# A latent attention block whose softmax reciprocals go through DRAM, with its closing steps tied to places in the engines' queues

## The chip, the cores and the metric

The kernel runs on one core of a Trainium2 chip. The metric is the device time of one execution in microseconds (us). The kernel before takes 1403.3 us, the median of three runs from 1401.08 to 1404.21. The core's engines are named as the profile names them: PE (TensorE, matrix products; PEld is its weight load), DVE (VectorE), ACT (ScalarE), POOL (GpSimd) and SP (SyncE, which here only issues DMAs). Each engine takes its instructions in the order of its own queue; semaphores make it wait for the others.

## What is computed

One layer of a bidirectional encoder over S = 2048 tokens of width 1024. One input projection feeds two groups of mixers: gated linear attention in chunks, forward and backward, and latent attention with a low-rank key and value and a rotary part. Their outputs, side by side, go through one output projection; a scaled residual and a layer norm follow. The part that the change touches is the second:

```python
def mla_branch(c_q, c_kv, k_rope, gate, positions, q_norm_g, w_uq, kv_norm_g, w_ukv):
    ...
    kv = (rms_norm(c_kv, kv_norm_g) @ w_ukv).reshape(B, S, MLA_HEADS, MLA_D_NOPE + MLA_DV)
    ...
    q_rope = apply_rope(q[..., MLA_D_NOPE:], positions) * scale
    k_nope, v = kv[..., :MLA_D_NOPE], kv[..., MLA_D_NOPE:]
    ...
        s = (jnp.einsum('bqhd,bkhd->bhqk', qn, k_nope, preferred_element_type=jnp.float32)
             + jnp.einsum('bqhr,bkr->bhqk', qr, k_r, preferred_element_type=jnp.float32))
        p = jax.nn.softmax(s, axis=-1)
        return jnp.einsum('bhqk,bkhv->bqhv', p.astype(v.dtype), v)
    ...
    return o * jax.nn.silu(gate)
```

There are 4 heads, 2048 queries and 2048 keys; a key has 128 numbers without position and 64 rotary ones, a value 128.

## The kernel before, in words

Most products are split to keep close to float32 at the speed of fp32r: a matrix A is a high part in float32r (A rounded by a copy on ACT, `hi`) and a low part (A minus its high part, on DVE or POOL, `lo`), and `mm3` makes three fp32r matmuls of them, high by high, high by low and low by high (L82 to L84). A plain float32 matmul is one call and appears as two rows.

The span has four stages. Up to about 385 us, `sweep_a` projects the 16 chunks of 128 tokens for the linear attention and runs its backward scan. On the way it makes the cos and sin tables of the rotary part (`rope_tables`), which lie in a pool that lives as long as the kernel. From about 385 to 400, `late_gates` loads the weights of the next projection (`wzr`, eight DMAs) and builds the remaining gates. From about 395 to 676, `sweep_c` makes the latents, the queries, the gates and the forward scan in eight steps of two chunks; its first matmuls of the scan (Ob, L792) follow on the first projections (ipm). It leaves queries in DRAM (`qh_s`, `ql_s`, `rh_s`, `rl_s`), gates in `gm_s`, the other group's outputs in `oa_s`. From about 676, `attention` (L894) runs 16 blocks: for each of 4 groups of 512 queries, each of 4 heads. The output projection of 16 chunks (`OutProj`, L1085) overlaps the last blocks and then runs alone to the end.

A block handles 512 queries of one head against all keys, in 8 pairs of key tiles (2 x 128 keys, against 512 columns of queries).

- `s_pair` (L929): ten fp32r matmuls make the scores of a pair in PSUM (L937 to L941; two buffers of two banks). ACT copies them to SBUF (L943), DVE keeps a running maximum over the pairs (L948).
- `maxima` (L951): DVE folds the two halves, PE transposes four times (mx, L958), DVE takes the maximum over the partitions (L960), and PE transposes it back, spread over all partitions (mb, L963), into a bank of the pool pM.
- `pv_pair` (L967): DVE subtracts mb (L970), ACT takes the exponential (L971). ACT and DVE or POOL split it into ph and pl (L65, L71), PE multiplies by the latent values into the bank o (L82 to L84; in mode "n" with one plain float32 matmul, L988). POOL adds the exponentials up in acc (L984). PV_MODE "dpdpndpd" says who makes pl for each of the 8 pairs: DVE (d), POOL (p), or nobody (n).
- `finish` (L1000): ACT copies o to osb (L1004), POOL folds acc (L1006). PE transposes the fold (sx, L1010), DVE sums it over the partitions and takes reciprocals (L1012, L1013), PE transposes those back, spread (r, L1017), DVE multiplies osb by r (L1018). PE multiplies by the head's value matrix wv (y, L1021), DVE multiplies by the gate (gma, L1023, loaded by L926 a block ahead), and the product is stored to `ob_s` (L1024).

Three pairs after the scores of a block have ended (LEAD = 3), its `pv_pair` steps begin, beside the scores of the next block. `finish` is a generator of four pieces; `todo` and FIN = (0, 2, 4) say after which later `pv_pair` each piece is emitted.

The order in each engine's queue isn't that of the program: the framework orders the instructions of each engine by a list schedule over their dependencies and buffers. `after` (L72 and on) pins the instructions made in it behind a given one. In `pv_pair` such a pin puts a pair's acc behind pl on POOL in block 0 alone (L983). The pools of PSUM hold two banks for mb (pM), one for o (pO), one for mx, sx, r and y (pX) and four for the scores (pS). `OutProj` takes its banks from pS and from pM (L1050, L1135). SP issues the loads of q (`fetch`, L911), of gma (`start`, L923) and of wo (L1038) in its queue's order.

The matrix wv is loaded and scaled in `setup_q` (L244), before the attention.

Of the kernel before, what the change touches and what calls it, by code (L numbers as in the profile page):

```python
# [9 lines left out]
F32 = mybir.dt.float32  # L10
F32R = mybir.dt.float32r
# [45 lines left out]
class K:  # L57
# [22 lines left out]
    def mm3(self, out, ah, al, bh, bl, start=True, stop=True):  # L80
        mm = self.nc.tensor.matmul
        mm(out, ah, bh, start=start, stop=False)  # L82
        mm(out, ah, bl, start=False, stop=False)  # L83
        mm(out, al, bh, start=False, stop=stop)  # L84
# [66 lines left out]
    def run(self):  # L151
        tc, nc, ins = self.tc, self.nc, self.ins
        with ExitStack() as top:
# [10 lines left out]
            self.oa_s = [dp.tile([P, H, P], F32, name=f"oa_s{c}") for c in range(NCH)]  # L164
            self.ob_s = [dp.tile([P, H, QB], F32, name=f"ob_s{b}") for b in range(NQB)]
# [5 lines left out]
            self.wv = cp.tile([P, H * P], F32, name="wv")  # L171
            self.cos = cp.tile([P, NCH, 32], F32, name="cosT")
            self.sin = cp.tile([P, NCH, 2, 32], F32, name="sinT")
# [35 lines left out]
    def setup_q(self, w1, ps):  # L209
# [15 lines left out]
        nc.sync.dma_start(self.wv, ins["wv"])  # L225
# [18 lines left out]
        nc.scalar.activation(self.wv, self.wv, AF.Copy, scale=self.gkv_c[:, 0:1])  # L244
# [48 lines left out]

    def rope_tables(self, hpi):
# [6 lines left out]
        V.tensor_scalar(self.sin[:, :, 0, :], self.sin[:, :, 1, :], -1.0, None, ALU.mult)  # L301


    def sweep_a(self):
        tc, nc, ins, cp = self.tc, self.nc, self.ins, self.cp
        with ExitStack() as ctx:
# [16 lines left out]
            hpi = wp.tile([P, 1], F32, name="hpi")  # L323
            nc.scalar.preload_act_table_set(EXP_LN)
# [260 lines left out]
    def late_gates(self):  # L585

        tc, nc, ins, bc = self.tc, self.nc, self.ins, self.bc
        self.xch = bc.tile([P, NK, 2, P], F32R, name="xch")
# [305 lines left out]
    def attention(self):  # L894
# [5 lines left out]
        with ExitStack() as ctx:  # L900
# [3 lines left out]
            pM = ctx.enter_context(tc.tile_pool(name="pM", bufs=2, space=PSUM, reuse_waits="tile"))  # L904
            pO = ctx.enter_context(tc.tile_pool(name="pO", bufs=1, space=PSUM, reuse_waits="tile"))
# [17 lines left out]
            def start(i):  # L923
                h, b = blocks[i]
                gm = bp.tile([P, QB], F32, tag="gm", name=f"gma{i}")
                nc.sync.dma_start(gm, self.gm_s[b][:, h])  # L926
                stt[i].update(gm=gm)

            def s_pair(i, j):  # L929
# [13 lines left out]
                d["copy"] = Ac.activation(s, ps, AF.Copy).ins  # L943
                src = s if i == 0 else ps
                if j > 0:
                    if j == 1:
                        d["rm"] = self.xfp.tile([P, 2, QB], F32, tag="xf", name=f"rm{i}")
                    V.tensor_tensor(d["rm"], src, d["s"][0] if j == 1 else d["rm"], ALU.max)  # L948
# [18 lines left out]
            def pv_pair(i, j):  # L967
# [10 lines left out]
                if j == 0:  # L978
                    d["acc"] = acc = bp.tile([P, 2, QB], F32, tag="acc", name=f"acc{i}")
# [257 lines left out]
```

## Time and profile before

| | us |
|---|---|
| median of 3 runs | 1403.3 |
| lowest and highest | 1401.08, 1404.21 |
| the profiled execution's own time | 1405.04 |
| its span in the trace | 1403.2 |
| PE busy | 1336.0 |
| DVE, ACT, POOL busy | 1021.5, 792.1, 693.1 |
| mean granted TensorE clock of the core | 0.983 |

The span runs from the first to the last instruction in the trace; the execution's own time holds some 2 us more. The prediction shows lines of several views. A row of a timeline has the start and the length of an instruction, its engine, line and operation, what it writes and reads, and in brackets how long its engine had been idle, with what ended that time. Matmuls overlap, and their lengths are modelled, so the distance between two starts says more than the length. A row of the waits has the engine and line that waited, what it waited for, the total, the number and the longest. The chain of waits follows the work back from its end, at each step to what released it. Line numbers are those of the kernel before; a number such as L71 can be that of a helper that many steps call.

### The profile page before, as it was taken

The numbers are of one execution on the slowest core, as the hardware profiler recorded it, in microseconds if no ns is written. First come the engines' busy times: TensorE is split into PE (matmuls) and PEld (weight loads), VectorE is DVE, ScalarE is ACT, GpSimd is POOL, SyncE is SP. The second block draws the span as 40 slices with busy tenths as digits, with TensorE's granted clock in tenths as the row PEclk, the third lists the DMA queues.
The fourth block names the chain that finished last, engine by engine and source line by source line (L and its number), as shares of the span: only waits on it lengthen the run. The fifth ranks groups of instructions, "written<-read, shape, count | busy, mean of one in ns | idle before, by whom it ended". The sixth has DMA issues, their size and how long they took to land.

```text
span 1403.2 us, 19420 instructions
## 1 busy us (share of the span) xinstructions
PE 1336.0 (95%) x7072; PEld 1139.4 (81%) x7072; DVE 1021.5 (73%) x1655; ACT 792.1 (56%) x1302; POOL 693.1 (49%) x353
## 2 busy tenths in 40 slices
PE   6899999999989999899999999999999999899997
PEld 6799999999888888888877777777777777678886
DVE  7747764545598777777588888888887789967665
ACT  6555556555565555655566777767666668521100
POOL 2432424232342222231088888888888888662210
PEclk9899999999999999999999999999999999999999
DMA  7222222222565555553821111111111002064432
GB/s 246 87 67 70 66 70 66 71 69 68 178 219 166 173 173 158 173 165 108 270 95 46 46 46 45 45 46 45 45 46 41 20 23 61 16 207 168 143 117 72
DMA packets 85297, 141.56 MB, mean 101 GB/s; under 512 B 9070, under 2 KB 38126, under 8 KB 85200
## 3 DMA queue, kind: packets, MB, share of 16 engines
q1 hardware_dynamic: 84528, 138.21, 31.7%
q0 software_dynamic: 672, 2.10, 0.4%
q8 instruction: 56, 0.92, 0.3%
q14 instruction: 41, 0.34, 0.1%
HBM read 89.95 MB, written 50.33 MB: 100 GB/s over the span
## 4 chain that ended last, share of the span: by engine, by line
PE 38%; DVE 11%; POOL 10%; issue 6%; ACT 5%; DMA 2%; SPq 0%; DVEq 0%; POOLq 0%; ACTq 0%
POOL acc L984 7%; POOL pl L71 3%; DVE MMb L71 2%; PE pS L940 2%; PE pS L941 2%; PE pS L937 2%; PE pS L939 2%; PE pS L938 2%; PE o L83 2%; PE o L84 2%; PE po L82 2%; PE po L84 2%; PE po L83 2%; PE pn L82 2%; PE pn L84 2%
## 5 line engine op out<-in xcount | busy, mean ns | idle before, releaser
L984 POOL TENSOR_TENSOR acc<-acc,s 128x1024 f32<-128x1024 f32 x96 | 269.8, 2811 | 13.4 <-ACT s L971 9.5
L943 ACT ACTIVATE s<-pS 128x1024 f32<-128x1024 f32 x128 | 131.2, 1025 | 108.8 <-PE pS L941 107.3
L970 DVE TENSOR_TENSOR s<-s,mb 128x1024 f32<-128x1024 f32 x128 | 152.9, 1206 | 12.3 <-PE mb L963 12.3
L65 ACT ACTIVATE ph<-s 128x1024 fp32r<-128x1024 f32 x112 | 118.2, 1055 | 44.8 <-PE o L84 44.5
L71 POOL TENSOR_TENSOR pl<-s,ph 128x1024 fp32r<-128x1024 f32 x43 | 109.4, 2544 | 68.4 <-ACT ph L65 68.4
L948 DVE TENSOR_TENSOR rm<-pS,rm 128x1024 f32<-128x1024 f32 x90 | 109.3, 1215 | 40.3 <-ACT s L943 40.3
L82 PE MATMUL ipa<-wah,xah 128*128 128x384 f32 (+1 forms) x384 | 130.8, 341 | 7.0 <-ACT wah L65 7.0
L971 ACT ACTIVATE s<-s 128x1024 f32<-128x1024 f32 x128 | 132.9, 1049 | 5.0 <-DVE s L970 5.0
L71 DVE TENSOR_TENSOR pl<-s,ph 128x1024 fp32r<-128x1024 f32 x69 | 116.3, 1685 | 16.3 <-ACT ph L65 16.1
L84 PE MATMUL ipa<-wah,xal 128*128 128x384 f32 (+1 forms) x384 | 125.9, 328 | 0.0
L83 PE MATMUL ipa<-wal,xah 128*128 128x384 f32 (+1 forms) x384 | 125.5, 327 | 0.2 <-DVE wal L71 0.2
L575 POOL TENSOR_TENSOR Us<-Us,cw 128x512 f32<-128x512 f32 x16 | 18.2, 1138 | 202.0 <-DVE Us L572 172.6
L937 PE MATMUL pS<-qh,ckvT_h 128*128 128x512 f32 x256 | 115.0, 449 | 0.0
L940 PE MATMUL pS<-rh,krs 128*128 128x512 f32 x256 | 101.4, 396 | 0.0
L939 PE MATMUL pS<-qh,ckvT_l 128*128 128x512 f32 x256 | 101.2, 395 | 0.0
L938 PE MATMUL pS<-ql,ckvT_h 128*128 128x512 f32 x256 | 101.0, 395 | 0.0
L941 PE MATMUL pS<-rl,krs 128*128 128x512 f32 x256 | 101.0, 395 | 0.0
L83 PE MATMUL o<-pl,vh 128*128 128x512 f32 x224 | 92.0, 411 | 7.0 <-DVE pl L71 4.0
L82 PE MATMUL o<-ph,vh 128*128 128x512 f32 x224 | 90.3, 403 | 0.8 <-ACT ph L65 0.8
L84 PE MATMUL o<-ph,vl 128*128 128x512 f32 x224 | 89.9, 401 | 0.0
L71 POOL TENSOR_TENSOR ol<-of,oh 128x512 fp32r<-128x512 f32 x32 | 44.5, 1403 | 81.0 <-PE po L84 63.0
L82 PEld LDWEIGHTS ipa<-wah,xah 128*128 128x128 f32 x384 | 73.5, 191 | 7.9 <-ACT wah L65 7.2
(311 smaller groups left out, 3900.4 us busy)
## 6 DMA issues: line engine op xcount, KB each, us to landing
xcf<-xT_dram SPq DMA_DIRECT2D x16, 512.0 KB, 4.0
xr<-x_dram SPq DMA_DIRECT2D x16, 512.0 KB, 3.8
out_dram<-rr SPq DMA_DIRECT2D x32, 256.0 KB, 2.1
xaf<-xT_dram SPq DMA_DIRECT2D x14, 512.0 KB, 4.2
SU<-su_s SPq DMA_DIRECT2D x16, 256.0 KB, 4.1
qdb<-qd_s SPq DMA_DIRECT2D x16, 256.0 KB, 4.5
oib<-oi_s SPq DMA_DIRECT2D x16, 256.0 KB, 2.6
ub<-u_s SPq DMA_DIRECT2D x16, 256.0 KB, 3.0
```

The costliest lines, as they stand in the source:

```text
L71: return e.tensor_tensor(dst, src, hi.bitcast(F32), ALU.subtract).ins
L82: mm(out, ah, bh, start=start, stop=False)
L83: mm(out, ah, bl, start=False, stop=False)
L84: mm(out, al, bh, start=False, stop=stop)
L937: mm(ps[:, e], kh, qh, start=True, stop=False)
L938: mm(ps[:, e], kh, ql, start=False, stop=False)
L939: mm(ps[:, e], kl, qh, start=False, stop=False)
L940: mm(ps[:, e], kr, rh, start=False, stop=False)
L943: d["copy"] = Ac.activation(s, ps, AF.Copy).ins
L970: V.tensor_tensor(s, s, d["mb"][:, None, :].to_broadcast([P, 2, QB]), ALU.subtract)
L971: Ac.activation(s, s, AF.Exp)
L984: d["pool"] = G.tensor_tensor(d["acc"], d["s0"] if j == 1 else d["acc"], s, ALU.add).ins
```

## The change

- **The close of a block.** The transposes r are gone. The reciprocals (rc, 128 x 4) are stored to DRAM (`r_s`, 512 numbers in a row) and loaded again, spread over all partitions (rb). o is split into a high part (ACT) and a low part (DVE), y is an `mm3` of three fp32r matmuls with a split wv, and the reciprocals are multiplied into the gate (gm*rb) in place of osb.
- **Ties.** `mm3` returns its last matmul. The last score copy on ACT (`cpi`), the last running maximum on DVE (`mxi`) and the last value matmul on PE (`pvi`) are kept, and the pieces of `finish` are pinned behind them: the high part of o behind cpi, sx behind pvi, y and gm*rb behind pvi and mxi. The fold is emitted ahead of the last pair's matmuls; the other pieces come 1 and 7 pairs later. A pair's acc is pinned behind pl for every "p" pair of all blocks.
- **Banks.** pM has one bank, pO two; `OutProj` takes its bank from pO.
- **Tables and weights.** cos and sin are made in a pool of `sweep_a`, stored to DRAM (`rope_s`, 768 KB) and loaded again in `late_gates`. wv is loaded, scaled and split at the start of the attention. gm is loaded in `finish`, in one buffer.

```diff
@@ -81,7 +81,7 @@
         mm(out, ah, bl, start=False, stop=False)
-        mm(out, al, bh, start=False, stop=stop)
+        return mm(out, al, bh, start=False, stop=stop).ins
 
@@ -162,15 +162,14 @@
             self.oa_s = [dp.tile([P, H, P], F32, name=f"oa_s{c}") for c in range(NCH)]
+            self.rope_s = [dp.tile([P, NCH, n, 32], F32, name=f"rope_s{n}") for n in (1, 2)]
+            self.r_s = [dp.tile([1, QB], F32, name=f"r_s{i}") for i in range(NQB * H)]
             self.ob_s = [dp.tile([P, H, QB], F32, name=f"ob_s{b}") for b in range(NQB)]
...
             self.gn_c = cp.tile([P, 1], F32, name="gn_c")
-            self.wv = cp.tile([P, H * P], F32, name="wv")
-            self.cos = cp.tile([P, NCH, 32], F32, name="cosT")
-            self.sin = cp.tile([P, NCH, 2, 32], F32, name="sinT")
             self.cw = cp.tile([P, NCH, 3, H], F32, name="cw")
@@ -222,7 +221,6 @@
         nc.sync.dma_start(wqT, ins["wqT"])
-        nc.sync.dma_start(self.wv, ins["wv"])
         nc.vector.tensor_scalar(gq, gq, QK_SCALE, None, ALU.mult)
@@ -241,7 +239,6 @@
             self.lo(self.wabs_l[:, ct], wa, self.wabs_h[:, ct], "pool")
-        nc.scalar.activation(self.wv, self.wv, AF.Copy, scale=self.gkv_c[:, 0:1])
         yield
@@ -291,6 +288,10 @@
 
+    def rope_tiles(self, pool, name):
+        self.cos = pool.tile([P, NCH, 32], F32, name=f"cos{name}")
+        self.sin = pool.tile([P, NCH, 2, 32], F32, name=f"sin{name}")
+
     def rope_tables(self, hpi):
@@ -299,6 +300,8 @@
         V.tensor_scalar(self.sin[:, :, 0, :], self.sin[:, :, 1, :], -1.0, None, ALU.mult)
+        nc.sync.dma_start(self.rope_s[0][:, :, 0], self.cos)
+        nc.sync.dma_start(self.rope_s[1], self.sin)
 
@@ -321,6 +324,7 @@
             hpi = wp.tile([P, 1], F32, name="hpi")
+            self.rope_tiles(wp, "T")
             nc.scalar.preload_act_table_set(EXP_LN)
@@ -585,6 +589,9 @@
         tc, nc, ins, bc = self.tc, self.nc, self.ins, self.bc
+        self.rope_tiles(bc, "C")
+        nc.sync.dma_start(self.cos, self.rope_s[0][:, :, 0])
+        nc.sync.dma_start(self.sin, self.rope_s[1])
         self.xch = bc.tile([P, NK, 2, P], F32R, name="xch")
@@ -901,8 +908,8 @@
             bp = ctx.enter_context(tc.tile_pool(name="bp", bufs=2, reuse_waits="tile"))
-            pM = ctx.enter_context(tc.tile_pool(name="pM", bufs=2, space=PSUM, reuse_waits="tile"))
-            pO = ctx.enter_context(tc.tile_pool(name="pO", bufs=1, space=PSUM, reuse_waits="tile"))
+            pM = ctx.enter_context(tc.tile_pool(name="pM", bufs=1, space=PSUM, reuse_waits="tile"))
+            pO = ctx.enter_context(tc.tile_pool(name="pO", bufs=2, space=PSUM, reuse_waits="tile"))
             pX = ctx.enter_context(tc.tile_pool(name="pX", bufs=1, space=PSUM, reuse_waits="tile"))
@@ -920,12 +927,6 @@
 
-            def start(i):
-                h, b = blocks[i]
-                gm = bp.tile([P, QB], F32, tag="gm", name=f"gma{i}")
-                nc.sync.dma_start(gm, self.gm_s[b][:, h])
-                stt[i].update(gm=gm)
-
             def s_pair(i, j):
@@ -940,12 +941,12 @@
                 s = sp.tile([P, 2, QB], F32, tag="s", name=f"s{i}_{j}")
-                d["copy"] = Ac.activation(s, ps, AF.Copy).ins
+                d["copy"] = self.cpi = Ac.activation(s, ps, AF.Copy).ins
                 src = s if i == 0 else ps
...
                         d["rm"] = self.xfp.tile([P, 2, QB], F32, tag="xf", name=f"rm{i}")
-                    V.tensor_tensor(d["rm"], src, d["s"][0] if j == 1 else d["rm"], ALU.max)
+                    self.mxi = V.tensor_tensor(d["rm"], src, d["s"][0] if j == 1 else d["rm"], ALU.max).ins
                 d["s"][j] = s
@@ -976,60 +977,77 @@
                 if j == 0:
-                    d["acc"] = acc = bp.tile([P, 2, QB], F32, tag="acc", name=f"acc{i}")
+                    d["acc"] = bp.tile([P, 2, QB], F32, tag="acc", name=f"acc{i}")
                     d["o"] = pO.tile([P, QB], F32, tag="o", name=f"o{i}")
...
                 else:
-                    with self.after(*([lo] if i == 0 and mode == "p" else [])):
+                    with self.after(*([lo] if mode == "p" else [])):
                         d["pool"] = G.tensor_tensor(d["acc"], d["s0"] if j == 1 else d["acc"], s, ALU.add).ins
+                if j == NP - 1:
+                    fin = finish(i)
+                    next(fin)
                 for e in range(2):
...
                     if mode == "n":
-                        mm(d["o"], self.vf[kt], s[:, e], start=(kt == 0), stop=(kt == NKT - 1))
+                        l = mm(d["o"], self.vf[kt], s[:, e], start=(kt == 0), stop=(kt == NKT - 1)).ins
                     else:
-                        self.mm3(d["o"], self.vh[:, kt], self.vl[:, kt], ph[:, e], pl[:, e],
-                                 start=(kt == 0), stop=(kt == NKT - 1))
+                        l = self.mm3(d["o"], self.vh[:, kt], self.vl[:, kt], ph[:, e], pl[:, e],
+                                     start=(kt == 0), stop=(kt == NKT - 1))
+                self.pvi = l
                 if j == NP - 1:
                     self.pv_end = d["act"], d["pool"]
-                    fin = finish(i)
-                    t = 8 * i + 7
-                    next(fin)
                     for dt in FIN:
-                        todo.setdefault(t + dt, []).append(fin)
+                        todo[NP * i + j + dt] = fin
+                elif NP * i + j in todo:
+                    next(todo.pop(NP * i + j))
 
             def finish(i):
+
+
                 h, b = blocks[i]
                 d = stt.pop(i)
-                osb = bp.tile([P, QB], F32, tag="osb", name=f"osb{i}", bufs=1)
-                Ac.activation(osb, d["o"], AF.Copy)
                 acc = d["acc"]
...
                 yield
+                oh = bp.tile([P, QB], F32R, tag="ofh", name=f"ofh{i}", bufs=1)
+                ol = bp.tile([P, QB], F32R, tag="ofl", name=f"ofl{i}", bufs=1)
+                with self.after(self.cpi):
+                    self.hi(oh, d["o"])
+                self.lo(ol, d["o"], oh)
                 x = pX.tile([P, 4, P], F32, tag="x", name=f"sx{i}")
-                for e in range(4):
-                    nc.tensor.transpose(x[:, e], acc[:, 0, e * P:(e + 1) * P], self.ident)
+                with self.after(self.pvi):
+                    for e in range(4):
+                        nc.tensor.transpose(x[:, e], acc[:, 0, e * P:(e + 1) * P], self.ident)
                 rc = bp.tile([P, 4], F32, tag="rc", name=f"rc{i}")
...
                 V.reciprocal(rc, rc)
-                yield
-                r = pX.tile([P, QB], F32, tag="x", name=f"r{i}")
-                for e in range(4):
-                    nc.tensor.transpose(r[:, e * P:(e + 1) * P], rc[:, e:e + 1].to_broadcast([P, P]), self.ident)
-                V.tensor_tensor(osb, r, osb, ALU.mult)
+                nc.sync.dma_start(self.r_s[i].rearrange("o (e p) -> p (o e)", p=P), rc)
+                gm = bp.tile([P, QB], F32, tag="gm", name=f"gma{i}", bufs=1)
+                nc.sync.dma_start(gm, self.gm_s[b][:, h])
+                rb = bp.tile([P, QB], F32, tag="rb", name=f"rb{i}", bufs=1)
+                nc.sync.dma_start(rb, self.r_s[i].to_broadcast([P, QB]))
                 yield
                 y = pX.tile([P, QB], F32, tag="x", name=f"y{i}")
-                mm(y, self.wv[:, h * P:(h + 1) * P], osb, start=True, stop=True)
-                ob = d["gm"]
-                V.tensor_tensor(ob, y, ob, ALU.mult)
-                nc.sync.dma_start(self.ob_s[b][:, h], ob)
+                hs = slice(h * P, (h + 1) * P)
+                with self.after(self.pvi, self.mxi):
+                    self.mm3(y, wv_h[:, hs], wv_l[:, hs], oh, ol)
+                    V.tensor_tensor(gm, gm, rb, ALU.mult)
+                V.tensor_tensor(gm, y, gm, ALU.mult)
+                nc.sync.dma_start(self.ob_s[b][:, h], gm)
                 yield
...
             nb = len(blocks)
-            todo, FIN = {}, (0, 2, 4)
+            todo, FIN = {}, (1, 7)
             wo = self.wo = []
...
             fetch(1)
-            start(0)
+            wv = bp.tile([P, H * P], F32, tag="ofh", name="wvf", bufs=1)
+            nc.sync.dma_start(wv, self.ins["wv"])
+            wv_h = bp.tile([P, H * P], F32R, name="wv_h", bufs=1)
+            wv_l = bp.tile([P, H * P], F32R, name="wv_l", bufs=1)
+            Ac.activation(wv, wv, AF.Copy, scale=self.gkv_c[:, 0:1])
+            self.hi(wv_h, wv)
+            self.lo(wv_l, wv, wv_h, "pool")
             for t in range(nb * NP + NP + LEAD):
@@ -1040,14 +1058,12 @@
                 if i < nb:
-                    if j == (4 if i else 4) and i + 1 < nb:
-                        start(i + 1)
-                        if i + 2 < nb:
-                            fetch(i + 2)
+                    if j == 4 and i + 2 < nb:
+                        fetch(i + 2)
                 t2 = t - NP - LEAD
...
                 if w == 3 - NP:
-                    op = OutProj(self, ctx, qp, bp, sp, pS, pM)
+                    op = OutProj(self, ctx, qp, bp, sp, pS, pO)
                     first = [op.load(0)]
@@ -1055,14 +1071,11 @@
                     pv_pair(*divmod(t2, NP))
-                    for fin in todo.pop(t2, ()):
-                        next(fin)
                 if w >= 1 and w <= NK:
...
             for t2 in sorted(todo):
-                for fin in todo[t2]:
-                    next(fin)
+                next(todo[t2])
             for o in first:
@@ -1132,7 +1145,7 @@
     def product(self, o):
-        o["ps"] = [self.ps2.tile([P, 512], F32, tag="mb", name=f"pn{o['c']}"),
+        o["ps"] = [self.ps2.tile([P, 512], F32, tag="o", name=f"pn{o['c']}"),
                    self.ps.tile([P, 2, 512], F32, tag="pS", name=f"po{o['c']}")[:, 0]]
```

## The prediction

> **What bounds the kernel now.** I read the page's head, then a table of stretches, the waits inside the attention, the chain of waits over one block and the matmul timeline at the places where the change takes something out. The head and the stretches:
>
> ```profile
> span 1403.2 us, 19420 instructions
> ...
> PE 1336.0 (95%) x7072; PEld 1139.4 (81%) x7072; DVE 1021.5 (73%) x1655; ACT 792.1 (56%) x1302; POOL 693.1 (49%) x353
> ```
>
> ```profile
> 740.00:1170.00 430.00, 426.95 (x1867) 329.71 (x1866) 350.26 (x325) 300.41 (x313) 362.88 (x144) 1.00 0.14 42
> ...
> 1190.00:1230.00 40.00, 33.03 (x133) 25.16 (x132) 39.08 (x27) 22.56 (x23) 28.60 (x12) 0.91 0.11 33
> ```
>
> In a stretch the columns are its length, then busy time of PE, PEld, DVE, ACT and POOL, granted clock, DMA share, GB/s. Between 740 and 1170 PE is busy 427 of 430 us at full clock: 13 attention blocks of 33.1 us, in which only fewer or sooner matmuls count. DVE has 350.3 and POOL 362.9, so both have some 5 us spare in a block. From 1190 to 1230 it is otherwise: DVE is full and PE has gaps, 7 us of them.
>
> What PE loses inside a block stands in the waits of 740 to 1170 (in total, times, longest; one per block) and in the matmul timeline (start, duration):
>
> ```profile
> PEld o L83 <- POOL pl L71: 8.6, 13, 1.6
> ```
>
> ```profile
> 1042.96 0.40 PE L84 MATMUL o<-ph,vl 128*128 128x512 f32 x1
> 1043.19 0.60 PE L1017 MATMUL r<-ident,rc 128*128 128x128 f32 x4
> 1043.55 0.48 PE L937 MATMUL pS<-qh,ckvT_h 128*128 128x512 f32 x1
> 1043.87 0.39 PE L938 MATMUL pS<-ql,ckvT_h 128*128 128x512 f32 x1
> ...
> 1049.65 0.39 PE L82 MATMUL o<-ph,vh 128*128 128x512 f32 x1
> 1050.20 0.50 PE L83 MATMUL o<-pl,vh 128*128 128x512 f32 x1 [0.16 <-POOL pl L71]
> 1050.54 0.40 PE L84 MATMUL o<-ph,vl 128*128 128x512 f32 x1
> ...
> 1051.24 0.39 PE L84 MATMUL o<-ph,vl 128*128 128x512 f32 x1
> 1051.46 1.02 PE L1021 MATMUL y<-osb,wv 128*128 128x512 f32 x2
> 1051.92 0.79 PE L937 MATMUL pS<-qh,ckvT_h 128*128 128x512 f32 x1
> 1052.55 0.39 PE L938 MATMUL pS<-ql,ckvT_h 128*128 128x512 f32 x1
> ```
>
> Ends are modelled, so I count start to start: an undisturbed 512-column matmul takes 0.232. From 1042.96 to 1043.87 lie two of them and the r transposes: 0.91 - 0.46 = **0.44 us**. From 1049.65 to 1050.54 lie two, and 0.89 - 0.46 = **0.43 us** is the wait for POOL's pl. From 1051.24 to 1052.55 lie two and the fp32 y: 1.31 - 0.46 = **0.84 us**. The block then adds up: 122 x 0.2322 = 28.33, the four fp32 matmuls of the "n" pair 1.71, mx 0.44, mb 0.50, sx 0.44, r 0.44, y 0.84, wait 0.43: 33.13, the block's measured period.
>
> **Part 1: r by DMA, y in three fp32r matmuls.** r's 0.44 goes. y becomes 3 x 0.232 = 0.70, 0.14 less. ACT is as before: its copy of o (0.60) becomes the high part. DVE loses osb*r (0.67, the mean of 13) and gains the low part of o and gma*rb. For the latter two I take the 0.67-0.70 of DVE's other 128x512 operations in this stretch. The high end is DVE's row for pl: 1.64 on average for twice the size where the fastest is 1.2, as an operation of POOL runs beside it; so up to 1.0 each. DVE's 26.9 us per block become 27.6 (at most 28.3) of 32.1. Followed through the queue with these durations, the tightest points are the running maxima of pairs 4 and 5 ahead of the next scores, 1.8 us early. So I cost DVE at nothing; delays over 1.8 us in the queue would cost PE each us in full.
>
> **Part 2: the round trip of rc.** The trace has no store in 4-byte pieces. Its nearest rows: the loads of gma and stores of ob_s land in 2.4 to 3.0 us, gkv_c and gn_c (loads, 128 pieces of 4 bytes) in 2.5 and 2.2, gq (8-byte pieces) in 3.2, pos_i in 5.5. rc has 512 pieces of 4 bytes. Two trips are 5 to 11 us. The cover: reciprocal at about 1076.8 of a block that begins at 1069, gma*rb tied behind the last maximum at about 1098.6: 21.8 us, hidden. SP waits at the store for rc and at the load of rb for the store; what stands behind it are q loads, due a block later. The gma load, issued between the two, waits in its one buffer for the ob_s store of the block before, some 30 us old. Cost nothing, high end as in rival C. The Trainium skill, "DMA: Bandwidth & Descriptors" (Specifications), says that transfers under 512 bytes are read-modify-write and off line rate; it gives no time for it and speaks against this step. The 2.2 to 3.2 us of the loads in 4- and 8-byte pieces show little of it; no row here shows such a store.
>
> **Part 3: pl ahead of acc on POOL.** Now POOL runs acc, acc, pl, acc x3, pl, acc x2, fold, pl (chain of waits):
>
> ```profile
> 1042.01 3.27 POOL acc L984
> 1045.54 2.17 issue
> 1047.70 2.45 POOL pl L71
> ```
>
> pl_3 sits behind an acc that could wait. With pl first it can end at least 2 us ahead of its matmul; the accs move back by up to 2.5, and POOL's idle time per block, 4.2, takes that; fold and sx follow by the same order. The 0.43 goes. If the fold were late instead, sx would wait on PE: at worst the same 0.43.
>
> **Part 4: banks and ties.** The one mb bank: the last subtraction reading it ends at 1047.0, the next mb transposes are at 1060.2, 13 us. The second o bank is needed: the old one was free at 1036.1, 2 us before the first o matmul at 1038.1, and the high and low parts now read it until about 1.5 us after the next o begins. With two, nothing waits. The order of the last matmuls and sx is unchanged, y moves to a place in PE's queue where its operands are some 15 us old.
>
> Per block 0.44 + 0.14 + 0.43 = 1.01; **13 x 1.01 = -13.1 us.** Blocks 14 and 15 are in the tail. Block 13's share there: -0.5.
>
> **Part 5: outside the loop.** *Entry of sweep C:* PE waits 2.83 us for Ob's operand at 400.6, and from 405.60 to 408.97 its 256-column matmuls stand 0.21 apart instead of 0.115, some 1.6 us more. In the new order four ipm matmuls of the next chunk stand before Ob (0.8 us) and its loads are reordered; against that 512 KB more net are moved at 382 to 400, where 305 GB/s are moving (1.7 us), and the sin table's load waits for a DVE operation at 383. Bounds -3.4 (both losses gone, 1 us left over) to +2; I take **-1.5**. *wv at the attention's start:* its load stands where gma's stood (landed in 4.3), and ACT has its scaling and high part (0.6 each) before the score copies which the third score pair needs. With 4.3 this is **+1.0**; 0 with 2.4, +2.5 with the 5.9 of the load behind it.
>
> *Tail.* Before:
>
> ```profile
> 1217.17 0.40 PE L82 MATMUL o<-ph,vh 128*128 128x512 f32 x1
> 1221.56 0.79 PE L83 MATMUL o<-pl,vh 128*128 128x512 f32 x1 [4.00 <-DVE pl L71]
> ```
>
> After these 4 us of idle time the next matmuls start at 1222.15, 1222.58 and 1223.01: 0.43 apart, not 0.23, until 1225.4. The same follows the idle 2.85 at 720.9 and 2.98 at 1191: a gap of about 2.8 us or more costs its own length and some 1.7 to 3 us of half rate. In the new order ACT's high part of o for block 15 stands behind the conversions of output chunk 4, which wait for loads (the second runs at 1243.24 now), and only four pn matmuls stand between sx and y. So y, 0.84 late now, waits from 1240.75 to 1244.35, 3.6 us. Followed to where that output chunk ends: +1.8, and 1.7 of half rate: **+3.5**, bounds 0 (scheduled loads land earlier) and +5. In the middle of the tail DVE's weight low parts now wait for POOL behind its accs: **+1.0**, bounds -4 (the gap of 4 us closes) and +3. From 1247 PE is full and carries each delay to the end. The Trainium skill, "TensorE: Matmul & The Clock Gate" (Part 1), puts the drop to half rate at an idle window of about 3.4 us and the return at about 3.4 us busy. Here gaps of 2.83 to 2.98 already bring it, so the measurement decides; by the page a y wait that came out under 3.4 would cost 1.7 less, and the sum be 1392.0.
>
> **Sum:** -13.1 - 0.5 - 1.5 + 1.0 + 3.5 + 1.0 = -9.6. The profiled execution's own time of 1405.04 (span 1403.2) becomes 1395.4; it lay 1.74 over the median of 1403.3, so the prediction is **1393.7**. The added up bounds of the parts outside the loop are -7.9 to +12.0 beside my +3.5 (block 13 among them); they hardly fall to one side together, and half the distance each way gives 1388 to 1398. The rivals B and D widen that upward.
>
> **Rivals.** *A, larger gain:* the Ob gap and the 4-us tail gap close, and y(15) is in time. -13.6 - 3.4 + 1 + 0 - 2 = -18 at the far end and about -14 halfway: 1385 to 1391, say 1389. For it: reordered loads, pl ahead of acc. Against: the queue orders of ACT at y(15). *B, DVE becomes the bound:* its low part of o and gma*rb meet POOL operations and go to 1.0 or more, the maxima come late and half of the block's gain is lost: +6.6, about 1400. For it: pl on DVE is 1.2 to 2.1 beside POOL. Against: 4 us spare in a block. *C, slower:* the 4-byte store and its load take over 21.8 us. Then gma*rb, waiting at the head of DVE's queue, holds the next block's subtractions, after 1.8 us of slack PE too. It decides from 23.6 us; 15 blocks pay each us more; over 24.3 the gain is gone, and at 25 it is 15 x 1.4 = 21 - 9.6 = +11.4, 1414.7. For it: 512 pieces in an unmeasured form, and SP's own wait. Against: 2.5 for 4-byte loads, a ninth of the cover. *D, it doesn't do what it says:* pl remains late as POOL is late for other reasons (acc 2.4 to 3.3 beside DVE): 0.43 x 13 = 5.6 less, 1399.
>
> **Chances.** Forecast 0.52 (1391 to 1397.5), A 0.18, B 0.10, C 0.10, D 0.10. The range 1387 to 1402 leaves out C and A's far third. A measurement of this kernel can tell 0.2%, 2.8 us, from no change: faster is below 1400.5. The forecast, A, and half each of B and D, which lie around that bound, give 0.80; their other halves 0.10 for the same; C 0.10 for slower.
>
> **What would show it.** The block's period in 740 to 1170 falls from 33.13 to 32.1, no r rows, three y rows 0.23 apart, no PE wait for POOL pl (13 times now). DVE busy near 0.86 of the stretch. rb's landing within 11 us of the reciprocal, and no DVE wait for it. A PE wait for DVE's low part of o or ACT's high part near 1230, 3 to 4 us. No gap at Ob of 2.8. It is wrong if PE waits inside the blocks for DVE's rm or s, or the period stays above 32.6.

## The result, and the profile after

The changed kernel takes 1419.9 us, the median of 4 runs (1417.8 to 1425.7), beside 1403.8 for the kernel before (four runs here): 1.2% slower, a ratio of 1.0123 with an interval of 1.009 to 1.0157. The forecast was 1393.7, 0.7% faster, with a range up to 1402. The profiled execution took 1425.7 (span 1423.8), some 6 us above the median of the others, so the profile's distances are a little larger than those of the medians.

The first look is at the page's head and the stretch from 740 to 1170 (columns as before):

```profile
PE 1331.4 (94%) x7024; PEld 1138.0 (80%) x7024; DVE 1058.8 (74%) x1671; ACT 790.9 (56%) x1303; POOL 693.0 (49%) x354
```

```profile
740.00:1170.00 430.00, 415.13 (x1816) 324.91 (x1815) 374.10 (x334) 296.50 (x310) 366.02 (x144) 1.00 0.19 48
```

PE has less work, as forecast, but idles 14.9 of 430 us, where it had idled 3.1. From one mx to the next the block takes 33.50 us; before it was 33.13, and the forecast was 32.12 (33.13 less 1.01). The waits of that stretch name one line. All that PE lost for POOL's pl is gone, and this stands in its place:

```profile
PEld mx L959 <- DVE rm L956: 19.7, 12, 1.7
PE mx L959 <- DVE rm L956: 14.5, 12, 1.3
```

L956 is DVE's fold of the two halves of the running maximum (L955 before). Here it is in the timeline of the changed kernel, DVE first, then POOL, then PE:

```profile
1056.68 1.22 DVE L949 TENSOR_TENSOR rm<-pS,rm 128x1024 f32<-128x1024 f32 x1 [2.35 <-ACT s L944]
1057.94 2.85 DVE L956 TENSOR_TENSOR rm<-rm 128x512 f32<-128x512 f32 x1
```

```profile
1057.86 2.38 POOL L71 TENSOR_TENSOR pl<-s,ph 128x1024 fp32r<-128x1024 f32 x1
```

```profile
1060.85 0.65 PE L959 MATMUL mx<-ident,rm 128*128 128x128 f32 x4 [1.28 <-DVE rm L956]
```

DVE was in time: it had waited 2.35 us for the scores. But its fold began 0.08 us after POOL's pl of pair 6 and ended 0.55 us after that pl. It took 2.85 us for what takes 0.71 in the kernel before, where it met only the end of a shorter POOL instruction:

```profile
1057.15 0.71 DVE L955 TENSOR_TENSOR rm<-rm 128x512 f32<-128x512 f32 x1
```

```profile
1056.02 1.29 POOL L1006 TENSOR_TENSOR acc<-acc 128x512 f32<-128x512 f32 x1
1057.25 2.87 POOL L71 TENSOR_TENSOR pl<-s,ph 128x1024 fp32r<-128x1024 f32 x1
```

There the fold began while POOL's own fold had 0.16 us to run. It too ended 0.55 us after that instruction, and the pl behind it on POOL took 2.87 in place of 2.4. That POOL waited there for DVE in turn is read from these lengths.

The second loss is in the tail. Against the kernel before, the same matmuls stand 2.7 us later at the first mx, 1.4 earlier at the third, 3.3 later at the fifteenth (1158), 9.2 at the last sx (1240) and 20.3 from output chunk 5 on. Of SP's queue in the changed kernel there:

```profile
1255.81 0.38 SPq L1024 DMA_DIRECT2D r_s<-rc  x1
1256.64 0.33 SPq L1026 DMA_DIRECT2D gma<-gm_s  x1
1257.31 0.33 SPq L1136 DMA_DIRECT2D xr<-x_dram  x1
1264.48 0.32 SPq L1028 DMA_DIRECT2D rb<-r_s  x1
1264.90 0.38 SPq L1123 DMA_DIRECT2D of<-oa_s  x1
```

SP stands from 1257.6 to 1264.5 at the load of rb, since the store of the reciprocals lands only after 8.3 us (the median in the list of DMA issues; for 13 of the 16 the landing is recorded; rb then takes 5.6). The loads of the coming output chunks stand behind it. PE pays at two places, first for the high part of o on ACT, then in the wake of the late loads:

```profile
1255.03 0.79 PE L82 MATMUL y<-ofh,wv_h 128*128 128x512 f32 x1 [4.94 <-ACT ofh L65]
...
1282.74 0.50 PE L82 MATMUL pn<-woh,oh 128*128 128x512 f32 x1 [3.51 <-DVE rr L1161]
```

### The profile page after: what moved, and what is told of

It is laid out like the page before. It is cut to its first block, busy times and chain, and to the rows that moved or that the text cites. A ratio compares the mean times of both kernels' runs of the same rounds, so it can differ in the third digit from the quotient of the medians.

```text
span 1423.8 us, 19401 instructions
## 1 busy us (share of the span) xinstructions
PE 1331.4 (94%) x7024; PEld 1138.0 (80%) x7024; DVE 1058.8 (74%) x1671; ACT 790.9 (56%) x1303; POOL 693.0 (49%) x354
## 4 chain that ended last, share of the span: by engine, by line
PE 42%; DVE 18%; ACT 4%; issue 3%; DMA 3%; POOL 1%; SPq 0%; DVEq 0%; ACTq 0%; POOLq 0%
PE pS L938 3%; PE pS L940 3%; PE pS L941 3%; PE pS L939 3%; PE pS L942 3%; PE o L84 3%; PE o L82 3%; PE o L83 3%; DVE rm L956 3%; DVE MMb L71 2%; DVE rm L949 2%; PE po L83 2%; PE pn L82 2%; PE po L82 2%; PE pn L84 2%
## 5 line engine op out<-in xcount | busy, mean ns | idle before, releaser
L985 POOL TENSOR_TENSOR acc<-acc,s 128x1024 f32<-128x1024 f32 x96 | 263.3, 2743 | 13.9 <-ACT s L972 9.1
L71 POOL TENSOR_TENSOR pl<-s,ph 128x1024 fp32r<-128x1024 f32 x43 | 104.7, 2434 | 81.5 <-ACT ph L65 67.5
L938 PE MATMUL pS<-qh,ckvT_h 128*128 128x512 f32 x256 | 108.5, 424 | 2.6 <-ACT s L944 1.3
```

The source lines that it names most:

```text
L71: return e.tensor_tensor(dst, src, hi.bitcast(F32), ALU.subtract).ins
L938: mm(ps[:, e], kh, qh, start=True, stop=False)
L985: d["pool"] = G.tensor_tensor(d["acc"], d["s0"] if j == 1 else d["acc"], s, ALU.add).ins
```

## The experiments

Theory 1: a DVE operation that reads two operands in SBUF and starts while a POOL instruction runs gets through only when that instruction ends; the tie of pl ahead of acc shifted POOL's queue so that the maximum's fold falls right behind the start of such an instruction. Its rival: DVE has too much work since the change. Theories 2 and 3 are for the tail: SP's hold at the store, and ACT's order at block 15. Each time stands beside the kernel before on the same chip (1403.1 to 1404.9).

**Fold early.** In the changed kernel:

```diff
+                    if j == NP - 1:
+                        r = d["rm"][:, 0]
+                        V.tensor_tensor(r, r, d["rm"][:, 1], ALU.max)
+                        V.tensor_tensor(r, src[:, 0], r, ALU.max)
+                        self.mxi = V.tensor_tensor(r, src[:, 1], r, ALU.max).ins
...
-                V.tensor_tensor(rm[:, 0], rm[:, 0], rm[:, 1], ALU.max)
```

> The changed kernel, with the fold of the running maximum moved: the two halves of rm are folded before the last pair's scores arrive (at pair 7 DVE folds rm, then takes the maximum with each half of the scores, which lie in PSUM, as two 512-column operations). DVE does some 0.2 us more per block. Theory 1 (the fold L956 of the changed kernel runs 2.85 us in place of 0.71 because it starts 0.08 us after POOL's pl of pair 6, reads two operands in SBUF, and gets through only when POOL's instruction ends; PE's mx waits 1.3 us for it): mx is no longer late, the block's period falls from 33.5 to about 32.2, 13 x 1.3 = 17 us less than the changed kernel's 1419.9, so 1401 to 1406. Rival (DVE simply has too much work since the low part of o and gma*rb were added): no gain or a loss of 0 to 3 us, 1420 to 1423.

1406.9, 13 less than the changed kernel and 0.9 over the range expected; period 32.79, not 32.2. No wait of PE for mx is left in the list. Theory 1 holds for the fold, the rival doesn't: DVE is busier here (406 of 430 us). For the 0.6 that remains to 32.2 the trace shows the same collision at another place, a DVE pl of 3.42 us that starts 0.08 us after an acc, and PE waiting for running maxima behind it:

```profile
PE pS L938 <- DVE rm L955: 4.9, 12, 0.4
```

**pl of pair 6 behind the fold.**

```diff
+                w1 = bp.tile([P, 1], F32, tag="w1", name=f"w1_{i}", bufs=1)
+                self.w1i = G.tensor_copy(w1, rm[:, 0, 0:1]).ins
...
+                    with self.after(*([self.w1i] if j == 6 and mode == "p" else [])):
                         lo = self.lo(pl, s, ph, "pool" if mode == "p" else "dve")
```

> The changed kernel with one POOL instruction more per block: it copies one column of the folded maximum, and pl of pair 6 is tied behind it, so that POOL can't start this pl before the fold on DVE is through. POOL's chain becomes about 0.9 us later from there. Theory 1: the fold takes 0.7 us again, mx doesn't wait, period 32.2 to 32.4, 1402 to 1407. Rival (DVE's load or order): the fold and the period stay, 1420 or a little more, since POOL only has more to do.

1411.1, 9 less; period 32.86; the fold takes 0.69. DVE has the instructions of the changed kernel; only POOL's start was moved, by one instruction more. The time is 4 us above the range expected, again with PE waiting for running maxima, some 0.4 per block.

**The tie alone, on the kernel before.**

```diff
-                    with self.after(*([lo] if i == 0 and mode == "p" else [])):
+                    with self.after(*([lo] if mode == "p" else [])):
```

> The kernel before with the one line that ties a pair's acc behind pl on POOL for all blocks, nothing else. The prediction on record: the 0.43 us wait for pl goes and nothing else changes, period 32.7, 13 x 0.43 = 5.6 us less, 1398. Theory 1: pl of pair 6 then starts about 1.0 us ahead of the maximum's fold on DVE, which ends about 0.4 us after PE wants it; this eats the gain, period 33.0 to 33.3, 1402 to 1407, and the fold takes 1.5 to 2.5 us in the trace.

1408.8, a ratio of 1.0038 (1.0023 to 1.0053): slower, not the 1398 of the prediction's step, and 1.8 over the range of theory 1. Period 33.28; in the steady blocks the fold takes 1.91 to 1.97, begun 1.0 after a pl. So this line, which seemed a pure gain, costs time without the rest of the change.

**The changed kernel without the tie** (the same line back).

> The changed kernel without that line: acc is tied behind pl in block 0 only, as before. Then acc of pairs 6 and 7 and the fold of acc come ahead of pl of pair 6 on POOL, as before. Theory 1: the fold of the maximum falls on another POOL instruction or on a handover as in the kernel before; the 0.43 us wait for pl of pair 3 is back, period 32.5 to 32.9, 8 to 13 us less than the changed kernel, 1407 to 1412. Rival (DVE's load): period stays at 33.5 or gets worse by 0.4, 1420 to 1425.

1420.2, no gain: the expectation failed. Period 33.48. Time and period are those of the rival, so this run by itself doesn't speak against DVE's load; the runs before and the next one do. The fold doesn't escape here: it takes 2.3, begun inside an acc that ends some 1.8 later, and it ends 0.55 after that acc. It is the same collision with another POOL instruction.

**POOL in halves,** on the changed kernel: pl and acc as two instructions of 512 columns.

```diff
+        if eng == "half":
+            for a in range(2):
+                l = e.tensor_tensor(dst[:, a], src[:, a], hi[:, a].bitcast(F32), ALU.subtract).ins
...
+                        a0 = d["s0"] if j == 1 else d["acc"]
+                        for a in range(2):
+                            d["pool"] = G.tensor_tensor(d["acc"][:, a], a0[:, a], s[:, a], ALU.add).ins
```

> The changed kernel with every 1024-column POOL instruction of the blocks (pl and acc) issued as two of 512 columns, in the same order; the work is the same, POOL gets some 1.6 us more per block (its 512-column rows are 1.29, the 1024-column ones 2.42). Theory 1 (a DVE operation with two operands in SBUF that starts while a POOL instruction runs gets through only at that instruction's end): the longest such wait halves, the fold takes at most 1.3 + 0.6 = 1.9 us in place of 2.85, DVE's pl rows shrink as well, PE waits 0 to 0.4 us for it, period 32.2 to 32.8, 1400 to 1409. Rival 1 (POOL slows DVE by taking a share of SBUF's bandwidth while both run): the fold stays at 2.5 to 2.9 us beside POOL, period 33.5, 1420. Rival 2 (DVE's load): as rival 1, without the fold's length.

1402.2, 18 less than the changed kernel, and 0.9984 of the kernel before (0.9968 to 1.0), so hardly clear of it. The period is 32.06, where the prediction's sum had 32.12. By groups of that stretch the fold has gone from a mean of 2627 ns to 1409:

```profile
L960 DVE TENSOR_TENSOR rm<-rm 128x512 f32<-128x512 f32 x13 | 18.3, 1409 | 0.4
```

POOL does 407 us of work there in place of 366, and DVE 386 in place of 374; what fell is only how long one POOL instruction lasts. That excludes a shared bandwidth (rival 1) and DVE's load (rival 2).

**Reciprocals of the last block by PE.**

```diff
...
+                else:
+                    rb = pM.tile([P, QB], F32, tag="mb", name=f"r{i}")
+                    for e in range(4):
+                        nc.tensor.transpose(rb[:, e * P:(e + 1) * P], rc[:, e:e + 1].to_broadcast([P, P]), self.ident)
```

> The changed kernel; for the last of the 16 blocks alone the reciprocals don't go through DRAM but are spread by four PE transposes into the free bank of mb, as the kernel before does for all. Theory 2 (the store of 4-byte pieces takes 8.3 us to land, SP stands at the load of rb behind it for that long, and the loads of the output projection's chunks 5 and 6, which are queued behind, come late; PE then stands 3.5 us at 1282.7 and runs at half rate after it): that stand goes, with the half rate 4 to 7 us less, 1413 to 1416. Rival (the tail's loss is the wait of y for ACT alone, and SP's hold is hidden): 1419 to 1421.

1415.4, 4.5 less, as expected; the five runs lie between 1410.9 and 1418.3, so the size is known to a few us only. The stand for rr is gone from the trace; from chunk 3 on nothing is lost against the kernel before. Theory 2 holds for the tail.

**Rows of 512 bytes in the store.**

```diff
+                yield
+                rt = pX.tile([4, P], F32, tag="x", name=f"rt{i}")
+                nc.tensor.transpose(rt, rc, self.ident)
+                rw = bp.tile([4, P], F32, tag="rw", name=f"rw{i}", bufs=1)
+                V.reciprocal(rw, rt)
+                nc.sync.dma_start(self.r_s[i].rearrange("o (e p) -> (o e) p", p=P), rw)
...
+            todo, FIN = {}, (1, 2, 7)
```

The close has one piece more here, so the reciprocals come one pair later.

> The changed kernel; the sums are transposed by PE (128 x 4 to 4 x 128, one transpose per block), the reciprocal is taken on 4 x 128, and the store writes 4 pieces of 512 bytes in place of 512 of 4. Theory 2: the landing of the store falls from 8.3 us to 2 to 3 (the rows of other stores), the steady blocks don't change (33.5; the round trip of 14 us lay under 21.8 of cover; PE has 0.1 to 0.3 more), and in the tail SP comes free 5 to 6 us earlier: 2 to 5 less, 1415 to 1418. Rival (the time is a write and a read behind it at DRAM, whatever the pieces): landing 7 us or more, 1420 to 1423.

1414.9, 5 less; the steady period is still 33.50, so the long round trip was hidden in the blocks. Not all of the gain is the store's: in the profiles 3.3 of the 9.2 us that the tail gains lie ahead of the last sx, where the last fold took 0.68 in place of 2.83. The landing isn't recorded, but SP's queue shows that rb is issued 2.25 us after the store, not 8.67, and 1.2 after it in each of the first 13 blocks (in the changed kernel 8.1 to 10.3). The last block's rows:

```profile
1250.72 0.27 SPq L1028 DMA_DIRECT2D r_s<-rw  x1
1251.93 0.33 SPq L1030 DMA_DIRECT2D gma<-gm_s  x1
1252.55 0.33 SPq L1140 DMA_DIRECT2D xr<-x_dram  x1
1252.97 0.38 SPq L1032 DMA_DIRECT2D rb<-r_s  x1
```

**The high part of o first.**

```diff
-                    with self.after(*self.pv_end):
+                    with self.after(*self.pv_end, *([self.ofi] if c > 2 else [])):
```

Here `ofi` is the instruction that makes the high part of o.

> The changed kernel with one tie more on ACT: the conversions of output chunk 4 and later come behind the high part of o of block 15, in place of ahead of it. The prediction on record put the wait of y(15) at 3.6 us and its price at 3.5 with half rate; the trace of the changed kernel shows 4.94 us of idle PE there. Theory 3: this wait falls below 1 us, 4 to 6 us less, 1414 to 1417. Rival: PE then meets the late loads of chunks 5 and 6 behind SP all the same, and the gain is eaten there, 1418 to 1420.

1420.4, no gain. Theory 3 as I wrote it failed, its rival came true: y no longer waits, and PE stands at the late loads instead, 5.7 us where it was 3.5:

```profile
1274.53 0.77 PE L82 MATMUL pn<-woh,oh 128*128 128x512 f32 x1 [5.72 <-DVE rr L1161]
```

**POOL in halves, on the kernel before** (the edit of the fifth run).

> The kernel before with its POOL instructions of the blocks (pl and acc) issued as halves of 512 columns, nothing else. The split changed kernel has a period of 32.06 and 1402.2. Theory 1: in the kernel before PE waits for no DVE operation in the steady blocks, only 0.43 us for POOL's pl; DVE's pl rows (1.36, 1.77, 2.13) shrink, which PE doesn't see; period 32.8 to 33.2 and 1396 to 1404; so the split is worth much to the changed kernel (18 us) and little here. Rival (the split helps whatever the kernel): period falls by 1 us or more here as well, below 1393.

1419.1, 1.2% slower, and the period is 34.41: the expectation failed, the rival too. Without the tie, pl stands behind several accs, and POOL's queue is on PE's path there, which I had left out. With halves PE's wait for POOL's pl is 1.2 us per block:

```profile
PE o L87 <- POOL pl L73: 15.9, 13, 3.3
```

**Halves, the last block by PE, and the high part first, together** (on the changed kernel), and the same with `W_POOL = (3,)`, which has DVE make the low part of the sixth output weight.

> Three edits on the changed kernel together: POOL's halves (1402.2 alone), the last block's reciprocals by PE transposes (alone 4 to 5 us less) and the high part of o of block 15 ahead of the conversions of chunk 4 (alone no gain, because PE then met the late loads behind SP; those are gone here). Theories 1 to 3 together: of the profile of the split kernel go the 3.7 us wait of y, the 3.0 us wait for rr, and half rate after them: 6 to 10 less, 1392 to 1397. Rival (each gain in the tail is given back at the next wait): 1399 to 1403.

> As e10, and the low part of the sixth output weight is made by DVE in place of POOL (W_POOL without 5). In the split kernel DVE stands 4.9 us at the head of its queue for POOL's low part of that weight, with pl and a subtraction of block 15 behind it, and PE stands 6.0 us at 1211.8 for pl. If that wait is the cause: 2 to 6 less than e10, 1388 to 1394. If DVE's work in that stretch is the bound (it gets 1.2 us more), no gain or up to 2 worse.

1394.1, 0.9931 of the kernel before (0.9913 to 0.9949), and 1392.7, 0.9919 (0.9903 to 0.9936): both beat both kernels. Over the halves alone the first gains 8. What the tie on ACT adds to the last block's reciprocals in that was not measured apart. The first of the two still has PE stand for a pl in the tail:

```profile
1208.19 0.80 PE L87 MATMUL o<-pl,vh 128*128 128x512 f32 x1 [6.05 <-DVE pl L75]
```

In the second that stand is gone, but the gain of 1.4 lies within the scatter of the runs (1391.0 to 1393.6, and 1391.6 to 1397.6), and a wait of 4.3 for the fold and one of 2.6 for rr stand in its trace.

**The tie and the halves, on the kernel before.**

> The kernel before with two edits: the tie of acc behind pl for all blocks (alone 1408.8: the fold ran 1.94 us) and POOL's halves (alone 1419.1: pl came later behind an acc, PE waited 1.2 us more per block). Neither the reciprocals by DMA, nor the banks, nor the moved closing steps. Theory 1: each edit takes away the other's wait: pl is early by the tie, the fold meets half instructions only; what is left over the split changed kernel's 32.06 is the r transposes 0.44 and y's 0.14, so a period of 32.6 to 32.8, 13 x 0.4 = 5 us less than before, 1397 to 1401, and about 7 us per run of blocks is what the reciprocals by DMA themselves bring. Rival (the closing steps and banks of the change are needed for the split to pay): period 33.1 or more, 1404 or more.

1401.4, a ratio of 0.9981 (0.9971 to 0.9992); period 33.07, not 32.6 to 32.8, and the time lies between the two forecasts, 0.4 over the one and 2.6 under the other. The two edits need each other: alone they cost 0.4% and 1.2%. PE still waits 0.3 for mx there. What the rest of the change (reciprocals by DMA, fp32r y, banks, moved closing steps) adds to this is the distance to 32.06, 1.0 us per block.

## Why the prediction was wrong

**The step that failed** is in part 1 and part 3: "Followed through the queue with these durations, ... I cost DVE at nothing", and, for the tie, "With pl first it can end at least 2 us ahead of its matmul; the accs move back". I moved POOL's instructions and kept the length that DVE's operations had beside the old order. The length of a DVE operation with two operands in SBUF is no constant of the operation. It depends on which POOL instruction runs when it starts. The rows for this were in the profile before. DVE's pl took 1.22 beside an idle POOL and 1.36, 1.77 and 2.13 in the same period, each of these until about 1.1 after the end of the POOL instruction it met:

```profile
1029.89 1.22 DVE L71 TENSOR_TENSOR pl<-s,ph 128x1024 fp32r<-128x1024 f32 x1
...
1049.10 2.13 DVE L71 TENSOR_TENSOR pl<-s,ph 128x1024 fp32r<-128x1024 f32 x1 [0.66 <-ACT ph L65]
```

```profile
1031.14 2.42 POOL L984 TENSOR_TENSOR acc<-s,s 128x1024 f32<-128x1024 f32 x1 [4.19 <-ACT s L971]
...
1047.70 2.44 POOL L71 TENSOR_TENSOR pl<-s,ph 128x1024 fp32r<-128x1024 f32 x1
```

I read them as a spread and put it into bounds, in place of asking which POOL instruction each would meet after the change. The fold was costed at its old 0.71, and no bound was taken for it. The price against the forecast period: 33.50 - 32.12 = 1.38 per block, 18 us in 13 blocks. The fifth run's period of 32.06 gives it back. In all folds of the changed kernel's steady blocks the end lies 0.55 us after the end of the POOL instruction that was running. The prediction had named its sign of being wrong, PE waiting inside the blocks for DVE's rm, and this sign came.

The blocks are only half of the miss. In the two profiles the changed kernel ends 20.6 us later, where the sum had 9.6 earlier, a miss of 30.2. Up to the second mx 3.2 of it arise. The 13 periods from there to the fifteenth mx took 0.6 us more, where the sum had 13.1 less: 13.7. (The first of these periods fell from 36.78 to 32.71, the twelve others missed 16.8.) From the fifteenth mx to output chunk 5 the changed kernel loses 17.0, where the terms of the tail gave 4.0 (-0.5 + 3.5 + 1.0): 13.0. The last 0.3 come behind it. So the second step that failed is these tail terms: part 2 looked at what stands behind SP's wait in the loop alone, and the collisions of DVE with POOL in the tail had no term.

The Trainium skill, "SBUF — State Buffer" (SBUF: two separate sides; Who interferes with whom), states this rule: DVE and GpSimd share a pair of ports; a `tensor_tensor` on DVE with both inputs in SBUF contends with GpSimd's reads, and whichever starts first holds the pair for the whole instruction. The traces agree: 2.85 behind a pl of 2.38 begun 0.08 earlier, 1.41 on the mean with halves. Operations with an operand in PSUM are unmoved: the low part of o (o is in PSUM) took 0.68 in each of the 13 blocks, although an acc ran beside it.

```profile
L956 DVE TENSOR_TENSOR rm<-rm 128x512 f32<-128x512 f32 x13 | 34.2, 2627 | 0.4
...
L71 DVE TENSOR_TENSOR ofl<-o,ofh 128x512 fp32r<-128x512 f32 x13 | 8.8, 680 | 0.0
```

**Point by point.**

- *r, y and the wait for pl, 1.01 per block:* right. No r rows; y's three rows 0.23 apart (1033.45, 1033.68, 1033.91); no PE wait for POOL's pl. The halved kernel's 32.06 is this sum.
- *Round trip, 5 to 11 us:* mis-sized, 8.3 + 5.6 = 13.9, and still below the cover of 21.8; DVE never waits for rb in the blocks. Rival C didn't occur. The nearest rows misled: loads in pieces of 4 bytes (2.2 to 2.5) say nothing of stores. In the blocks the gma load is issued ahead of the store, not behind it, and 2.3 to 2.8 us after the ob_s store whose buffer it takes, not some 30; it cost nothing.
- *"What stands behind it are q loads, due a block later":* right for the blocks, wrong for the last one, where the output chunks' loads stand there. Sixth and seventh run: 4.5 to 5 us on the medians.
- *Banks:* right, no wait for mb or o.
- *y(15), 3.6 us of wait, +3.5:* the wait was 4.94, for the named reason. Its price can't be had alone, since the eighth run moves the wait to the late loads.
- *wv, +1.0:* a wait of 1.3 for the score copy, at 690.5.
- *Entry of sweep C, -1.5:* the wait of 2.83 for Ob is gone as forecast, but 1.1, 1.6 and 1.5 appear at 416 to 424, for wabs, ckv and krs. At the last Ob the changed kernel's profile stands 1.1 later than that of the kernel before; the nine experiments with the same code up to there stand 0.4 to 4.1 earlier, the three others with the code of before 1.0 earlier to 1.3 later. So on the mean of these profiles the term has the right sign and about its size, with a scatter of 2 us around it. The rate of 305 GB/s in its working is about that of 382 to 390 (304); over 382 to 400 the profile shows 234, by which the 512 KB would cost 2.2, not 1.7.
- *Middle of the tail, +1.0:* from the fifteenth mx to the last sx the profile loses 5.9 us. DVE and POOL collide there as in the blocks (gma*rb took 1.89 and 2.85 in the thirteenth and the fifteenth close, 0.68 in the others). The wait that the term named, DVE for POOL's low part of a weight, is 1.15 us in the changed kernel's trace, about as forecast; the collisions had no term. With POOL in halves (fifth run) that wait is 4.87, and the stretch loses 8.0. In the last pair of runs on the changed kernel, which differ only in who makes the low part of the sixth output weight, it loses 7.9 with POOL and 1.9 with DVE. So shorter POOL instructions alone don't bring this stretch back.
- *Rival B, "DVE becomes the bound",* was near in its symptom, but with a wrong mechanism and price: 0.10 for a half loss of the gain. It named "pl on DVE is 1.2 to 2.1 beside POOL", and took it for a question of load. *Rival D* didn't occur: PE no longer waits for POOL's pl. Nor did *A*: the wait at Ob went, the gap of 4.00 in the tail became 2.81, but y(15) was late.

The tail's loss can be divided further by the traces. From the last sx to the last matmul PE has the same 672 matmuls of the output projection left in all kernels. This takes 154.8 us in the kernel before (154.8 to 155.2 in the three experiments on it) and 166.0 in the changed one. It takes 160.7 to 163.2 in the five experiments that keep SP's hold at a store of 4-byte pieces, 160.1 with rows of 512 bytes (no stand for rr, but y waits 4.86), and 156.1 with the last block's reciprocals by PE (no stand for rr, y waits 2.40). With the halves and the tie on ACT besides it takes 154.8 (158.4 where DVE makes the weight's low part, with the wait of 2.6 for rr). So that part, 11.1 us, is PE's stands for y and for rr with the matmuls 0.43 apart that follow each (1255.6 to 1259.9 and 1284.0 to 1287.4). Both stands go in the combined run. What stays open is how the part ahead of the last sx, 5.9 us, divides among collisions and other waits in the changed kernel itself, since each removed wait is partly met again at the next.

## What to carry to other kernels

Before costing a reordered queue on GpSimd or VectorE, mark every VectorE operation that reads two SBUF operands, and ask which GpSimd instruction is running when it will start; in these traces its length was about its own plus that instruction's rest. Such a collision can be defused by shorter GpSimd instructions, by one operand left in PSUM, or by an earlier place for the operation that PE waits for. Each needs a run: the halves gave the changed kernel 18 us and cost the kernel before 14. A round trip through DRAM that is hidden in the loop still holds its DMA queue; look at what stands behind it after the last iteration.

## What the runs showed of the hardware

- A store from 128 partitions to 512 pieces of 4 bytes in DRAM landed in 8.3 us (median of the 13 recorded). The same 2 KB as 4 rows of 512 bytes let the next dependent load go 1.2 us after the issue. Loads of 128 pieces of 4 bytes landed in 2.2 to 2.8 in the two profiles. The Trainium skill, "DMA: Bandwidth & Descriptors" (Specifications), states the read-modify-write below 512 bytes. These stores agree with it; but the rows have not only larger pieces, they also are 4 in place of 512, and no run here tells the two apart.
- Splitting POOL's instructions of 1024 columns in two cost POOL 41 us in 13 blocks (366 to 407), and saved 18 us of the changed kernel.
- A collision, once met, came back in every later block: from the fifth fold to the fifteenth each began 0.07 to 0.15 us behind POOL's pl. That the waiting PE keeps this phase is an inference.
